# x laid out by features on the host, the first projection fed earlier, later group statistics, and one convolution tap on ACT

## The chip, the core and the metric

The kernel runs on one core of a Trainium2 chip. The core has a matrix engine (TensorE, PE; PEld is its weight load), a vector engine (VectorE, DVE), an activation engine (ScalarE, ACT), a general engine (GpSimd, POOL) and a sync engine (SP), whose queue issues most loads. Each engine runs its instructions in the order in which they were laid down. Engines share an on-chip memory; matmuls write into eight PSUM banks. The metric is the device time of one execution in microseconds (us), here the median of three.

## What is computed

One layer over a sequence of 2048 tokens with 1024 features. The input is normalised and modulated by a conditioning vector, projected once into three groups of heads (a gated LRU, HGRN2 and Mamba-2 SSD), and all results go through one output projection, a gate, the residual and a last normalisation:

```python
mod = cond @ w_ada[l] + b_ada[l]
shift, scale, gate = jnp.split(mod, 3, axis=-1)
h = rmsnorm(x, norm_w[l]) * (1.0 + scale[:, None]) + shift[:, None]
u = h @ w_in[l]
a_x, a_g, hg_q, hg_f, hg_i, hg_g, ssd_z, ssd_xbc, ssd_dt = jnp.split(u, split_points, axis=-1)
xa = causal_conv(a_x, ...)                  # width 4, also over ssd_xbc
ya = rg_lru(xa, ...) * jax.nn.silu(a_g)
yb = rmsnorm(hgrn2_chunked(...), hg_norm_w[l]) * jax.nn.silu(hg_g)
yc = rmsnorm(ssd_chunked(...) * jax.nn.silu(ssd_z), by 2 groups)
y = jnp.concatenate([ya, yb, yc], axis=-1) @ w_out[l]
x = x + gate[:, None] * y
return rmsnorm(x, final_norm_w)
```

## The kernel before

Tokens are taken in four blocks of 512 (`tb` 0 to 3), features in eight tiles of 128 (`KT`). The program has two halves, blocks 0 and 1, then 2 and 3. In each half the stages follow one another: the HGRN heads (projections `ps_f`, `ps_q`, `ps_g`, `ps_v`), the SSD groups (`ps_bc`, `ps_x`, `ps_z`), and four LRU stages `i` = 0 to 3 (`ps_lx`, `ps_lg`, then the gates `ps_r`, `ps_i`). After both halves the output stage runs over 16 token tiles and four families of input features, `po` on PE (line 1095).

Every projection is done in a pair of numbers, a high and a low part, in three passes over eight feature tiles: 24 matmuls of 512 tokens for one 128-column block (`proj_mm`, `PASSES`). A weight tile is loaded as `raw`; `split` (line 139) makes `w` or `wt`, high on ACT and low on POOL.

The h tiles are made by `h_tile` (line 307). A tile of x is loaded with tokens on the partitions (`load_x`, line 274), its squares are summed on ACT (`norm_stats`, line 282), it is scaled by the reciprocal root (`norm_scale`, line 293), transposed by four PE matmuls into `ps_xt` (line 311), modulated on ACT (`hf`), cast on DVE to the high part and subtracted on DVE or POOL to the low part (`ht`).

The modulation has 16 numbers per partition in `gsc`. `mod_dma` (line 412) loads 256-column pieces `wta` of `w_ada`; `mod_acc` (line 421) multiplies and adds them on DVE into `macc`; `mod_col` (line 434) sums over the partitions by a matmul with ones into `psm` and adds the constants.

Order. PE's order is written out by hand. For the startup the string `PROG` (line 40) lists the steps: D, A and C are loads, accumulation and column sums of one modulation tile, X loads a block of x, S and N its statistics and scaling, H builds h tile k of block tb, M runs the three projections on it, w and W load and split the first weights, K loads constants (`consts`, line 452), B starts the other weight loads. Later `weave` (line 366) mixes a list of projection pieces with branches, generators which hand over after each step, by given weights: `pend` holds the branches that run beside the next stage. The other engines' orders come from a scheduler that places each operation when the program is built. ACT operations made by `sact` (line 151) keep their written order. The loads on the sync queue use eight lanes: a load waits for the one eight before it.

`conv` (line 494) copies the last three columns of the block before (`halo`) into `craw` on DVE, the projection into it on ACT, and then runs four taps on DVE (one `tensor_scalar`, line 500, and three multiply-adds, line 72) into `cacc`. `stats` (line 509) sums the squares of a group over partitions by `pq` matmuls (line 513) after POOL has added up `acc`. `lru` (line 810) makes the gate matmuls `ps_r` and `ps_i` for the two blocks, the first pair in the PSUM tag "sc" and the second in "ms"; between them it hands over with weight `L0` = 0.01. In LRU stage 2 of the first half block 2 of x is loaded and scaled (`norm_gen`, line 869), in stage 3 block 3; `h_build` (line 876) makes block 2's h tiles beside stage 3 and block 3's beside the first `ps_v` of the second half. `finish` (line 1116) multiplies a token tile by the gate on POOL, adds the residual and squares.

PSUM tags: "mm" has three banks, "sc" two, "oy" one, "ms" two. Slots of the on-chip memory: 32 temporary tiles, 8 weight slots (`wp`), 16 h slots (`hp`).

## Time and profile before

| | |
|---|---|
| time, median of 3 | 1758.56 us (1758.46 to 1760.5) |
| the profiled execution | 1758.94 us |
| its span | 1757.2 us |
| mean granted PE clock | 0.983 |
| PE busy | 1675.2 us (95%) |
| DVE, POOL, ACT busy | 1149.1, 836.8, 622.3 us |

The span runs from the first to the last recorded instruction of the core; the execution's own time is a little longer. Busy time counts instructions that do work, not waits, branches or the issue of loads. "Granted clock" is the share of full speed at which PE was clocked. In a timeline a row gives start, length, engine, line, operation, output and inputs by name, the tile, the number of instructions, and in brackets how long the engine was idle before it and what released it.

### The profile page before, as it was taken

The page shows a single profiled execution, that of the slowest core. Times are in us where ns is not written, and L with a number is a line of the kernel's source. Part 1 is how long each engine was busy: PE and PEld are TensorE (multiplying, and loading weights), DVE is VectorE, ACT ScalarE, POOL GpSimd, SP SyncE. Part 2 cuts the span into 40 slices and gives each one's busy share as a digit, 9 for nine tenths or more (in the row PEclk, how much of TensorE's full clock was granted, in tenths as well). Part 3 has the DMA queues.
Part 4 walks back from the last instruction along what each step waited for, and adds up shares of the span by engine and source line. Part 5 has one row for each costly group of instructions (what it writes and reads, how often), then busy time and mean ns, then how long its engine had stood idle before and what let it go on. Part 6 is the DMA issues. An engine that isn't in the chain of part 4 may idle for free. (4 is left out here: it accounts for less than half of the span.)

```text
span 1757.2 us, 29508 instructions
## 1 busy us (share of the span) xinstructions
PE 1675.2 (95%) x11448; PEld 1371.7 (78%) x11448; DVE 1149.1 (65%) x2260; ACT 622.3 (35%) x1164; POOL 836.8 (48%) x681
## 2 busy tenths in 40 slices
PE   3899999999999999899999999999999799999998
PEld 2688877788788877788988788788877577888886
DVE  6955756788878947726755778878869636333333
ACT  5322322233333367622322333333446533222221
POOL 3433344265636665424334346634757546333333
PEclk9899999999999999999999999999999899999999
DMA  8612011111202232311120111201224444333332
GB/s 242 166 52 61 26 37 32 34 45 49 73 19 61 66 109 85 89 40 41 29 59 26 37 37 49 84 13 53 69 80 142 135 129 141 94 96 96 92 91 70
DMA packets 178988, 129.52 MB, mean 74 GB/s; under 512 B 13856, under 2 KB 153632, under 8 KB 178848
## 3 DMA queue, kind: packets, MB, share of 16 engines
q1 hardware_dynamic: 142512, 102.72, 20.8%
q10 hardware_dynamic: 33936, 17.04, 3.2%
q0 software_dynamic: 2400, 7.87, 1.1%
q8 instruction: 90, 1.47, 0.4%
q14 instruction: 50, 0.41, 0.1%
...
## 5 line engine op out<-in xcount | busy, mean ns | idle before, releaser
L1095 PE MATMUL po<-wo,yy 128*128 128x512 f32 x1512 | 356.1, 397 | 4.0 <-POOL yy L69 3.4
L69 POOL TENSOR_TENSOR w<-raw,w 128x512 fp32r<-128x512 f32 x158 | 227.2, 1456 | 247.6 <-ACT w L66 232.4
L1095 PEld LDWEIGHTS po<-wo,yy 128*128 128x128 f32 x1512 | 285.5, 189 | 74.5 <-POOL yy L69 4.7
L72 DVE SCALAR_TENSOR_TENSOR cacc<-craw,col,cacc 128x512 f32<-128x512 f32 x192 | 201.9, 1051 | 2.1
L323 PE MATMUL ps_x<-ht,w 128*128 128x512 f32 x768 | 191.2, 397 | 0.0
L323 PE MATMUL ps_z<-ht,w 128*128 128x512 f32 x768 | 189.6, 399 | 0.0
L323 PEld LDWEIGHTS ps_z<-ht,w 128*128 128x128 f32 x768 | 141.9, 188 | 33.6 <-issue 2.1
L323 PEld LDWEIGHTS ps_x<-ht,w 128*128 128x128 f32 x768 | 143.1, 189 | 30.1
L72 DVE SCALAR_TENSOR_TENSOR o<-po,rstd,o 128x512 f32<-128x512 f32 x64 | 47.5, 751 | 116.8 <-PE po L1095 108.0
L69 POOL TENSOR_TENSOR hg_k<-hg_k,hg_t 128x256 f32<-128x256 f32 x80 | 59.5, 759 | 127.1 <-PE ps_sA L551 63.5
L329 PE MATMUL ps_v<-vw,ht 128*128 128x264 f32 x768 | 105.3, 295 | 4.6 <-DVE ht L69 3.6
L66 ACT ACTIVATE w<-raw 128x512 fp32r<-128x512 f32 x158 | 91.4, 625 | 46.0 <-issue 22.3
L323 PE MATMUL ps_f<-ht,w 128*128 128x512 f32 x384 | 101.0, 410 | 6.4 <-DVE ht L315 5.9
L69 POOL TENSOR_TENSOR yy<-yr,yy 128x512 fp32r<-128x512 f32 x61 | 78.5, 1306 | 59.7 <-ACT yy L66 44.2
L323 PE MATMUL ps_bc<-ht,w 128*128 128x512 f32 x384 | 106.0, 417 | 0.0
L329 PEld LDWEIGHTS ps_v<-vw,ht 128*128 128x128 f32 x768 | 99.0, 195 | 7.6 <-DVE ht L69 4.6
L323 PE MATMUL ps_lx<-ht,w 128*128 128x512 f32 x384 | 99.8, 411 | 0.0
L323 PE MATMUL ps_q<-ht,w 128*128 128x512 f32 x384 | 99.7, 407 | 0.0
L69 POOL TENSOR_TENSOR s_ce<-s_ce,cacc 128x512 f32<-128x512 f32 x64 | 96.9, 1532 | 0.8 <-ACT s_ce L66 0.8
L323 PE MATMUL ps_lg<-ht,w 128*128 128x512 f32 x384 | 93.7, 398 | 0.0
L323 PE MATMUL ps_g<-ht,w 128*128 128x512 f32 x336 | 91.9, 408 | 0.0
L323 PEld LDWEIGHTS ps_lx<-ht,w 128*128 128x128 f32 x384 | 72.8, 191 | 20.7 <-issue 5.5
...
## 6 DMA issues: line engine op xcount, KB each, us to landing
...
```

The lines of the kernel that those rows point to most:

```text
L66: S.activation(o, i, f, **kw)
L69: e.tensor_tensor(o, a, b, op=op)
L72: V.scalar_tensor_tensor(o, a, s, b, op0=op0, op1=op1)
L323: d_ = PE.matmul(ps, b.hl[wl][:, k, :], ht[:, hl, :], start=(k == 0 and n == 0), stop=(k == KT - 1 and n == 2))
L329: d_ = PE.matmul(ps[:, 0:264], ht[:, hl, c * P:(c + 1) * P], b.vw[k // 4][wl][:, k % 4, :], start=(k == 0 and n == 0), stop=(k == KT - 1 a ...
L1095: PE.matmul(pss[t, n], yys[u, t][yl][:, k4, :], wts[4 * fam + k4][wl][n], start=(k4 == 0 and i == 0), stop=(k4 == 3 and i == 2))
```

## The change

The diff has ten parts.

1. The host hands over x also transposed (`x_t`), the modulation weights in 2-KB rows (`w_mod`) and the gate's columns apart (`w_gate`). `load_x` reads `x_t` with features on the partitions, so PE transposes nothing. `h_tile` becomes: `h_pre` on DVE (x times the modulation scale times a row `rb` of reciprocal roots), ACT adds the shift and writes the high part, DVE makes the low part. `rb` is made by four 128x128 matmuls against the identity (`norm_rows`, `ps_rb`) and a copy on ACT.
2. Statistics of blocks 0 and 1: ACT squares the eight tiles, DVE adds them up (`xsq`), four matmuls with ones give the sums (`ps_ss`). For blocks 2 and 3 `norm_stats` reads x a second time (16 loads `xr`) and squares it on ACT in LRU stages 0 and 1 of the first half.
3. `mod_acc` on DVE is replaced by `mod_mm`: eight matmuls per modulation tile with `condz` (32 columns, one of them not zero) in four column groups, and a copy on ACT.
4. `PROG` is new. Block 0's x lies in weight slots that are not in use yet, the squares in h slots; U steps are matmuls of ones by ones (`warm`); the first half of the first weights is split on DVE.
5. `conv`: the copies of the halo and the fourth tap move to ACT, which reads PSUM twice; DVE keeps three multiply-adds.
6. `late`: the statistics of an SSD group run one stage later.
7. The first run of the second half holds `ps_v`, `ps_f` and `ps_q` of block 2, then those of block 3; the branches beside it are in parts (`some`), and `norm_gen` hands over three times.
8. The last LRU hands over with weight 5, so that 45 instead of 3 `po` matmuls stand between its two pairs; both pairs use "sc".
9. `finish` multiplies by the gate on DVE.
10. `split` can run on DVE and be told what to follow.

At the start PE's order was this (`psm` are the column sums of the modulation, `ps_xt` transposed x, `ps_f`, `ps_q` and `ps_g` projections of one h tile):

```order
L438 MATMUL psm<-ones,macc 128x1 x2
L311 MATMUL ps_xt<-ident,xt 128x128 x4
L323 MATMUL ps_f<-ht,w 128x512 x3
L323 MATMUL ps_q<-ht,w 128x512 x3
L323 MATMUL ps_g<-ht,wt 128x512 x3
L438 MATMUL psm<-ones,macc 128x1 x2
L311 MATMUL ps_xt<-ident,xt 128x128 x12
L323 MATMUL ps_f<-ht,w 128x512 x3
L323 MATMUL ps_q<-ht,w 128x512 x3
L323 MATMUL ps_g<-ht,wt 128x512 x3
```

and is now this (`warm` are matmuls of ones, `ps_ss` and `ps_rb` the sums and the row of roots):

```order
L997 MATMUL warm<-ones 128x512 x8
L440 MATMUL psm<-wta,condz 32x256 x8
L997 MATMUL warm<-ones 128x512
L449 MATMUL psm<-ones,macc 128x1 x2
L997 MATMUL warm<-ones 128x512 x2
L311 MATMUL ps_ss<-ones,xsq 128x1 x4
L320 MATMUL ps_rb<-ident,xsc 128x128 x4
L440 MATMUL psm<-wta,condz 32x256 x8
L997 MATMUL warm<-ones 128x512
L449 MATMUL psm<-ones,macc 128x1 x2
L440 MATMUL psm<-wta,condz 32x256 x8
L338 MATMUL ps_f<-ht,w 128x512 x3
```

Eight matmuls against `wta` now stand on PE for each modulation tile, four matmuls per h tile are gone, and the first projection stands behind three modulation tiles.

On DVE, in the startup, a stretch before reads like this (`macc` is the accumulation of a modulation tile, `gsc` its two columns, `ht<-hf` the cast to the high part):

```order
L72 SCALAR_TENSOR_TENSOR macc<-wta,cond,macc 128x256
L315 CAST ht<-hf 128x512
L72 SCALAR_TENSOR_TENSOR macc<-wta,cond,macc 128x256
L69 TENSOR_TENSOR gsc<-psm,col 128x1
L72 SCALAR_TENSOR_TENSOR gsc<-psm,col 128x1
L72 SCALAR_TENSOR_TENSOR macc<-wta,cond,macc 128x256
L69 TENSOR_TENSOR gsc<-gsc,col 128x1
```

No `macc` is left there now. At the passage from block 0 to block 1 the order is now this (`xsq` are the sums of squares of block 1, `aneg` is made of the constants `rowp`, the last load of `consts`; `xt<-xt,gsc,rb` is `h_pre`, `ht<-xt,gsc,ht` the low part, `hg_q` and `hg_f` gate operations of block 0):

```order
L480 COPY cs_576<-p_575 128x4
L483 TENSOR_SCALAR e_574<-col 128x4
L488 TENSOR_SCALAR aneg<-aneg 128x16
L305 TENSOR_TENSOR xsq<-xsq 128x512
L72 SCALAR_TENSOR_TENSOR xt<-xt,gsc,rb 128x512
```

and, some 15 operations on a few columns later, this:

```order
L72 SCALAR_TENSOR_TENSOR xt<-xt,gsc,rb 128x512
L69 TENSOR_TENSOR sp_p<-sp_p,sp_w 128x4
L72 SCALAR_TENSOR_TENSOR xt<-xt,gsc,rb 128x512 x7
L136 TENSOR_SCALAR sp_p<-sp_p 128x4
L72 SCALAR_TENSOR_TENSOR hg_q<-hg_q,omlb,ps_q 128x512
L533 TENSOR_SCALAR hg_f<-hg_f,omlb 128x512
L72 SCALAR_TENSOR_TENSOR ht<-xt,gsc,ht 128x512
```

All eight `h_pre` of block 1 stand ahead of its first low part, with two operations of block 0 between.

At the end of the first half PE's order was this (stage 3 of the LRU, then `ps_v` of block 2):

```order
L311 MATMUL ps_xt<-ident,xt 128x128 x4
L323 MATMUL ps_lg<-ht,w 128x512 x6
L815 MATMUL ps_r<-cacc,wab 128x512
L816 MATMUL ps_i<-cacc,wab 128x512
L329 MATMUL ps_v<-vw,ht 128x264 x6
L815 MATMUL ps_r<-cacc,wab 128x512
L816 MATMUL ps_i<-cacc,wab 128x512
L329 MATMUL ps_v<-vw,ht 128x264 x24
L311 MATMUL ps_xt<-ident,xt 128x128 x4
L329 MATMUL ps_v<-vw,ht 128x264 x6
L311 MATMUL ps_xt<-ident,xt 128x128 x4
L329 MATMUL ps_v<-vw,ht 128x264 x12
```

and is now this:

```order
L338 MATMUL ps_lg<-ht,w 128x512 x24
L826 MATMUL ps_r<-cacc,wab 128x512
L827 MATMUL ps_i<-cacc,wab 128x512
L344 MATMUL ps_v<-vw,ht 128x264 x6
L320 MATMUL ps_rb<-ident,xst 128x128 x4
L344 MATMUL ps_v<-vw,ht 128x264 x90
L338 MATMUL ps_f<-ht,w 128x512 x24
L338 MATMUL ps_q<-ht,w 128x512 x6
L826 MATMUL ps_r<-cacc,wab 128x512
L827 MATMUL ps_i<-cacc,wab 128x512
L338 MATMUL ps_q<-ht,w 128x512 x18
L344 MATMUL ps_v<-vw,ht 128x264 x96
```

The transposes are gone; a `ps_rb` stands between the `ps_v`, and the `ps_f` and `ps_q` of block 2 stand ahead of the `ps_v` of block 3 (x96).

The diff, cut to its core:

```diff
-PROG = ("D0 A00 X0 D1 A10 w0 A01 S0 X1 N0013 A11 C0 H00v W0 M00 D2 S1 C1 H01v N10 H10 A20 D3 w1 "
-        "A30 A21 A31 H11v M01 C2 D4 N111g H02 M10 H12 M11 W1 C3 N01 A40 H03 A41 D5 M02 H13 M12 C4 "
-        "A50 H04 D6 A51 M03 A60 H14 D7 M13 C5 H05 H15 A61 M14 M04 C6 K A70 H06 M05 A71 H16v M15 "
-        "C7 B H07v H17 M06 M07 M16 M17")
+PROG = ("X0 D0 w0 D1 w1 D2 S0 U8 A0 U1 C0 U2 R0 W0 D3 A1 U1 C1 H00 D4 W1 A2 M00 C2 H01 D5 A3 M01 C3 H02 D6 A4 M02 C4 "
+        "H03 D7 A5 M03 C5 H04 X1 A6 M04 C6 H05 S1 A7 M05 C7 H06 K M06 H07 R1 B M07 H10 H11 M10 H12 M11 H13 M12 H14 M13 "
+        "H15 M14 H16 M15 H17 M16 M17")
...
-    def load_x(tb):
-        r = [[tmp("xt") for _ in range(2)] for _ in range(4)]
+    def load_x(tb, ts=None):
+        r = []
+        for k in range(KT):
+            t_ = ts[k // 2][:, k % 2] if ts else tmp("xt")
+            nc.sync.dma_start(t_, x_t[k * P:(k + 1) * P, tb * TB:(tb + 1) * TB])
+            r.append(t_)
...
+    def norm_stats(tb):
+        st = tmp("xst", (P, 2, 4), bufs=2)
         for n in range(2):
             for i in range(4):
                 r0 = tb * TB + i * P
-                nc.sync.dma_start(r[i][n], x[r0:r0 + P, n * TB:(n + 1) * TB])
-        return r
-
-    def norm_stats(xs):
-        st = tmp("xst", (P, 2, 4), bufs=2)
-        for n in range(2):
-            for i in range(4):
-                sq = tmp("xsq", (P, TB), BF16, bufs=1)
-                act(sq, xs[i][n], AF.Square, accum_out=st[:, n, i:i + 1])
+                xr = tmp("xr")
+                nc.sync.dma_start(xr, x[r0:r0 + P, n * TB:(n + 1) * TB])
+                act(xr, xr, AF.Square, accum_out=st[:, n, i:i + 1])
...
+    def norm_sum(xs, sqs):
+        a = sqs[0][:, 0]
+        for k in range(KT):
+            sq = sqs[k // 2][:, k % 2]
+            act(sq, xs[k], AF.Square)
+            if k > 0:
+                d_ = V.tensor_tensor(a, a, sq, op=ADD)
+        return a, d_.ins.name
+
+    def norm_cols(a):
+        ps = bank(ps_ms, "ms", "ps_ss")
+        for i in range(4):
+            PE.matmul(ps[:, i:i + 1], a[:, i * P:(i + 1) * P], ones[:, 0:1], start=True, stop=True)
+        st = tmp("xsc", (P, 4), bufs=2)
+        sact(st, ps[:, 0:4], AF.Sqrt, scale=1.0 / D, bias=epsc[:, 0:1])
+        V.reciprocal(st, st)
         return st
 
-    def norm_scale(xs, st, n, on_act=()):
+    def norm_rows(st):
+        ps = bank(ps_ms, "ms", "ps_rb")
         for i in range(4):
-            if on_act is G:
-                tt(G, xs[i][n], xs[i][n], st[:, 0, i:i + 1].to_broadcast([P, TB]), MUL)
-            elif i in on_act:
-                act(xs[i][n], xs[i][n], AF.Copy, scale=st[:, 0, i:i + 1])
-            else:
-                V.tensor_scalar(xs[i][n], xs[i][n], st[:, 0, i:i + 1], None, op0=MUL)
-
-    def norm_x(xs, on_act=()):
-        st = norm_stats(xs)
-        for n in range(2):
-            norm_scale(xs, st, n, on_act)
-
-    def h_tile(xs, k, dep=None, lo=G):
+            PE.matmul(ps[:, i * P:(i + 1) * P], st[:, i:i + 1].to_broadcast([P, P]), ident, start=True, stop=True)
+        rb = tmp("rb")
+        d_ = S.activation(rb, ps, AF.Copy)
+        return rb, d_.ins.name
+
+    def h_pre(xs, rb, k):
+        stt(xs[k], xs[k], gsc[:, 1, k:k + 1], rb, MUL, MUL)
+
+    def h_tile(xs, k, dep=None):
         ht = hp.tile([P, 2, TB], F32R, tag="h", name="ht")
-        ps = bank(ps_ms, "ms", "ps_xt")
-        for i in range(4):
-            d_ = PE.transpose(ps[:, i * P:(i + 1) * P], xs[i][k // 4][:, (k % 4) * P:(k % 4 + 1) * P], ident)
-            after(d_, dep)
-        hf = tmp("hf")
-        act(hf, ps, AF.Identity, scale=gsc[:, 1, k:k + 1], bias=gsc[:, 0, k:k + 1])
-        V.tensor_copy(ht[:, 0], hf)
-        tt(lo, ht[:, 1], hf, ht[:, 0], SUB)
+        after(S.activation(ht[:, 0], xs[k], AF.Identity, bias=gsc[:, 0, k:k + 1]), dep)
+        stt(ht[:, 1], xs[k], gsc[:, 0, k:k + 1], ht[:, 0], ADD, SUB)
         return ht
...
+            wt = tmp("wta", (P, 2, 2 * P))
+            nc.sync.dma_start(wt, w_mod[j, :, q * TB:(q + 1) * TB].rearrange("p (k c) -> p k c", k=2))
...
+    def mod_mm(j):
+        psm = bank(ps_ms, "ms", "psm")
+        for k in range(KT):
+            r = k % 4
+            PE.matmul(psm[32 * r:32 * r + 32, 0:2 * P], condz[:, k, :], mws[j][k // 2][:, k % 2],
+                      start=k < 4, stop=k >= 4)
+        mas[j] = tmp("macc")
+        act(mas[j][:, 0:2 * P], psm[:, 0:2 * P], AF.Copy)
...
     def conv(ps, wi, wname, bname, i):
         raw = tmp("craw", (P, TB + 3))
-        V.tensor_copy(raw[:, 0:3], halo[:, wi, :])
+        act(raw[:, 0:3], halo[:, wi, :], AF.Copy)
         act(raw[:, 3:], ps, AF.Copy)
-        V.tensor_copy(halo[:, wi, :], raw[:, TB:TB + 3])
         a = tmp("cacc")
-        V.tensor_scalar(a, raw[:, 0:TB], cc(wname, 4 * i), cc(bname, i), op0=MUL, op1=ADD)
-        for k in (1, 2, 3):
+        act(a, ps, AF.Identity, scale=cc(wname, 4 * i + 3), bias=cc(bname, i))
+        act(halo[:, wi, :], ps[:, TB - 3:TB], AF.Copy)
+        for k in range(3):
             stt(a, raw[:, k:k + TB], cc(wname, 4 * i + k), a, MUL, ADD)
...
-    def lru(i, tbs, xa, gs):
+    def lru(i, tbs, xa, gs, l0=L0):
         r, ig = {}, {}
         for n, tb in enumerate(tbs):
-            pool, tag = ((ps_sc, "sc"), (ps_ms, "ms"))[n]
+            pool, tag = ((ps_sc, "sc"), (ps_ms, "ms"))[n if l0 < 1 else 0]
...
-                yield L0
+                yield l0
...
+    def norm_gen(xs, st):
+        rb, _ = norm_rows(st)
         yield
+        for k in range(KT):
+            h_pre(xs, rb, k)
+            if k % 4 == 3:
+                yield
+
+    def some(g, n):
+        for w_ in itertools.islice(g, n):
+            yield w_
...
-                ps_ = pv(tbs[0])
                 if p == 0:
-                    brs = pend + [(h_build(tbs[1], xs_next, HTS[tbs[1]], hdep[tbs[1]]), 8)]
-                    run(ps_, brs)
-                    pend = []
-                    ps_ = pv(tbs[1])
+                    g_ = pend[0][0]
+                    run(pv(tbs[0]) + pf(wf, h, tbs[0]) + pq_(wq, h, tbs[0]),
+                        [(some(g_, 1), L0), (norm_gen(xs_next, xst[1]), 3),
+                         (h_build(tbs[1], xs_next, HTS[tbs[1]], hdep[tbs[1]]), 8), (some(g_, 9), 3)] + pend[1:])
+                    run(pv(tbs[1]) + pf(wf, h, tbs[1]) + pq_(wq, h, tbs[1]) + pg(wg, h, tbs[0]) + pg(wg, h, tbs[1]))
...
+            pend = [(ssd_bc(g, tb, bc[0, tb], bc[1, tb], dts[tb][1], bcg), 3) for tb in tbs] + late
+            late = []
...
-            pend += [(stats(acc[tb], 1 + g, tb), 2) for tb in tbs]
-        hdep = {}
+            late = [(stats(acc[tb], 1 + g, tb), 2) for tb in tbs]
+        hdep, xst = {}, {}
...
+            if i < 2 and half == 0:
+                xst[i] = norm_stats(2 + i)
             if i == 2 and half == 0:
                 xs_ = load_x(2)
-                pend += [(norm_gen(xs_), 1)]
+                pend += [(norm_gen(xs_, xst[0]), 3)]
...
-                    norm_x(xs_next)
...
+            l0 = 5 if i == 3 and half == 1 else L0
+            pend = [(lru(i, tbs, xa, gs, l0), 3 + l0)] + late
+            late = []
...
-            tt(G, o, o, gate[n], MUL)
+            tt(V, o, o, gate[n], MUL)
```

More of the change, by code (lines that the diff above doesn't have):

```diff
@@ L1 @@
+import itertools
 from contextlib import ExitStack
@@ L95, in trunk @@
     cond = cpool.tile([P, 8], F32, name="cond")
+    condz = cpool.tile([P, 8, 32], F32, name="condz")
     dhalf = cpool.tile([P, 8], F32, name="dhalf")
@@ L437, in mod_col @@
         for i in range(2):
-            PE.matmul(psm[:, i:i + 1], ma[:, i], ones[:, 0:1], start=True, stop=True)
-        tt(V, gsc[:, 0, j:j + 1], psm[:, 0:1], cc("b_shift", j), ADD)
+            PE.matmul(psm[:, i:i + 1], ma[:, i * P:(i + 1) * P], ones[:, 0:1], start=True, stop=True)
         stt(gsc[:, 1, j:j + 1], psm[:, 1:2], 1.0, cc("b_scale", j), ADD, ADD)
         tt(V, gsc[:, 1, j:j + 1], gsc[:, 1, j:j + 1], cc("norm_w", j), MUL)
+        tt(V, gsc[:, 0, j:j + 1], psm[:, 0:1], cc("b_shift", j), ADD)
     G.memset(wab, 0.0)
@@ L945, in trunk @@
                         for tb in tbs}
-                xsb, sts, u_ = {}, {}, None
+                xsb, sts, u_, dn, rn = {}, {}, None, None, None
+                sqs = [[hp.tile([P, 2, TB], F32, tag="h", name="xsq") for _ in range(4)] for _ in tbs]
+                x0s = [wp.tile([P, 2, TB], F32, tag="w", name="xt") for _ in range(4)]
                 for op_ in PROG.split():
                     o_, ar = op_[0], [int(c) for c in op_[1:] if c.isdigit()]
-                    e_ = V if op_[-1] == "v" else G
                     if o_ == "D":
@@ L970, in trunk @@
                         for b_ in WBL[0:3]:
-                            b_.parts(ar[0])
+                            b_.parts(ar[0], *((dn, V) if ar[0] == 0 else (rn, G)))
+                    elif o_ == "U":
+                        pu = bank(ps_ms, "ms", "warm", (P, 4, P))
+                        for _ in range(ar[0]):
+                            PE.matmul(pu, ones, ones.unsqueeze(1).to_broadcast([P, 4, P]), start=True, stop=True)
                     elif o_ == "K":
@@ L1195, in trunk @@
     tc_pe.__exit__(None, None, None)
-_INS = ["x", "w_ada", "w_in", "w_out", "wa", "wx", "cols", "rows", "ident", "tri", "masks", "onehot"]
+_INS = ["x", "x_t", "w_mod", "w_gate", "w_in", "w_out", "wa", "wx", "cols", "rows", "ident", "tri", "masks", "onehot"]
 def _arrays(inp):
```

85 lines of the change are left out of this document (38 added, 47 removed).

## The prediction

> **What bounds the kernel now.** I read the page first (busy shares), then the waits of the matrix engine PE, then busy time by windows, then PE's timeline at the places that these point to.
>
> ```profile
> PE 1675.2 (95%) x11448; PEld 1371.7 (78%) x11448; DVE 1149.1 (65%) x2260; ACT 622.3 (35%) x1164; POOL 836.8 (48%) x681
> ```
>
> PE is busy 1675.2 of the 1757.2 us of the span, so it is idle for 82.0 us. No other engine is near its limit over the whole span. Removing DVE or POOL work is therefore worth only the PE idle time that it ends. The view of PE's waits says who ends that idle time (total us, times, longest):
>
> ```profile
> PE psm L438 <- DVE macc L72: 14.6, 4, 10.6
> PE ps_xt L311 <- DVE xt L300: 10.8, 5, 7.4
> PE ps_r L815 <- DVE cacc L72: 8.3, 1, 8.3
> PE pq L513 <- POOL acc L69: 5.6, 4, 2.0
> PE po L1095 <- POOL yy L69: 3.4, 3, 2.5
> ```
>
> Almost all of it is in few places. Busy time of PE in windows (start:end, length, PE busy, weight loads, DVE, ACT, POOL, granted PE clock, DMA share, GB/s) shows where:
>
> ```profile
> 0.00:50.00 50.00, 19.98 (x66) 14.85 (x67) 32.23 (x68) 23.43 (x52) 16.07 (x19) 0.90 0.79 229
> ...
> 100.00:150.00 50.00, 50.00 (x593) 44.82 (x592) 24.41 (x53) 12.10 (x34) 18.60 (x20) 1.00 0.10 27
> ...
> 700.00:750.00 50.00, 43.38 (x270) 37.67 (x269) 37.92 (x60) 29.77 (x57) 23.24 (x17) 0.92 0.41 107
> 1350.00:1400.00 50.00, 41.06 (x158) 30.56 (x157) 40.01 (x46) 31.16 (x45) 32.02 (x24) 0.90 0.33 107
> ```
>
> A steady window is full at clock 1.00. Three stages are not: the startup (first 95 us), the passage from the first half to the second (690 to 752), and the last LRU before the output stage (1350 to 1400). There the clock falls as well. The sum goes stage by stage.
>
> **Startup, term 1: 14 us less.** The timeline of PE (start, length, line, operation; in brackets the idle time before):
>
> ```profile
> 10.56 1.01 PE L438 MATMUL psm<-ones,macc 128*128 128x1 f32 x4 [10.56 <-DVE macc L72]
> ...
> 25.98 0.80 PE L323 MATMUL ps_f<-ht,w 128*128 128x512 f32 x1 [5.94 <-DVE ht L315]
> ...
> 82.28 1.12 PE L311 MATMUL ps_xt<-ident,xt 128*128 128x128 f32 x4 [4.18 <-DVE gsc L72]
> ...
> 90.98 0.86 PE L323 MATMUL ps_f<-ht,w 128*128 128x512 f32 x3
> ...
> 92.36 0.85 PE L323 MATMUL ps_g<-ht,wt 128*128 128x512 f32 x3
> ```
>
> The first projection runs from 25.98 to about 93.1. Its 16 steps of three groups need 2.08 us each (from 90.98 to 92.36 are two groups, 0.69 each), 33 us in all; half the stretch is waiting on DVE, which computes the modulation (64 `macc` operations). The change gives that to PE and removes the transposes. What is late next is the data, then a row of DVE work. In the changed order on the sync queue the second block of x is the 54th large load; with 32 modulation tiles, 16 of x and 6 of weights, 256 KB each, 14.2 MB have to land. Rates, from the same view of windows:
>
> ```profile
> 10.00:20.00 10.00, 2.09 (x8) 1.54 (x8) 3.84 (x14) 7.46 (x20) 0.00 (x0) 1.00 1.02 314
> ...
> 24.00:26.00 2.00, 0.02 (x1) 0.02 (x1) 1.97 (x4) 1.94 (x5) 0.79 (x1) 1.00 1.04 392
> 30.00:36.00 6.00, 3.30 (x13) 2.22 (x12) 4.56 (x8) 0.78 (x1) 4.17 (x4) 0.94 1.01 267
> ```
>
> The 30:36 window carries modulation weights in 512-byte runs at 267 GB/s; 24:26 carries x in 2-KB runs at 392. The change makes the modulation runs 2 KB too, so I take 370 from between 314 and 392: 38.3 us, and with some 4 us before the stream starts it ends at 42.5 (41 to 49). The Trainium skill's page "DMA: Bandwidth & Descriptors" (Bandwidth) gives about 358 GB/s as the limit of one core from HBM; by it the stream would take 39.6 us and this term would be 1.3 us smaller. The 392 GB/s of the second row exceeds that figure, and the measurement decides.
>
> Behind that stream stand small loads: 8 loads are in flight, so `rowp` is issued only when x has landed. DVE's order has `aneg`, which needs `rowp`, ahead of the last square-sum of the second block. `rowp` takes 3.5 us to land (first row below), so the chain stands at 46.
>
> ```profile
> DMA to landing us min/median/max: 3.5/3.5/3.5
> ...
> L72 DVE SCALAR_TENSOR_TENSOR cacc<-cacc,dhalf,ps_y 128x512 f32<-128x512 f32 x32 | 23.5, 744 | 11.9 <-PE ps_y L783 11.9
> ...
> L151 ACT ACT_TABLE_LOAD x29 | 37.2, 1283 | 8.7 <-POOL l_gs L69 8.3
> ```
>
> From there: one addition, one h operation, a root with its table load (1.283), the row broadcast on PE and its copy on ACT, about 6 us to 52; then eight `h_pre` in a row by 0.72 to 0.744, 5.8 us, to 57.6; two gate operations ahead of the first `lo`, and that `lo`, 2 us, to 59.6. Eight steps of 2.08 plus some 2 us at half clock end at 78 to 79, against 93.1. Bounds: 72 if DVE's small operations slip by, 88 if the stream runs at 314 and the row of DVE work meets POOL; gain 5 to 21, taken 14.
>
> The new modulation matmuls (eight per step, 32 columns each, in four column groups) have no row of their own. Nearest: a 128x512 f32 matmul is two records, 0.43 apart (the last two rows).
>
> ```profile
> 104.01 0.76 PE L551 MATMUL ps_sA<-hg_q,hg_k 128*32 128x32 f32 x64
> ...
> 406.05 0.39 PE L783 MATMUL ps_y<-s_ce,s_st 128*64 128x128 f32 x4
> 406.27 0.39 PE L778 MATMUL ps_y<-s_m,s_xdt 128*64 128x128 f32 x4
> ...
> 421.36 1.05 PE L754 MATMUL ps_bx<-s_xw,s_btok 128*128 128x128 f32 x8
> ...
> 710.25 1.02 PE L815 MATMUL ps_r<-cacc,wab 128*128 128x512 f32 x2
> 711.11 1.02 PE L816 MATMUL ps_i<-cacc,wab 128*128 128x512 f32 x2
> ```
>
> 710.25 to 711.11 is 0.86 for 512 columns, so 0.43 for 256. One after another, eight cost 3.4 us; four at a time, 0.86. Halves do overlap: four records of 64 columns start 0.22 apart (0.055 each), where eight of 128 columns take 0.81 (0.10 each). So I take 0.86, which the loads of each step (4 of 256 KB, 2.8 us at 370) cover beside 2.08 of projection. The page "TensorEngine Tiling (Array Packing)" of the Trainium skill (Key Properties) says that a switch of tiling mode drains TensorE, which speaks against these 8 detours. The 100:150 window holds five groups of 32-column matmuls (the first is the 104.01 row) between projections, with PE busy 50.00 of 50: here the trace does not agree, a switch shows no idle time. By the trace a step costs 0.86; by the page each detour would add two drains of unknown length.
>
> **Passage to the second half, term 2: 13 us less.** PE's timeline:
>
> ```profile
> 697.82 1.11 PE L311 MATMUL ps_xt<-ident,xt 128*128 128x128 f32 x4 [3.90 <-ACT hf L66]
> 698.58 2.71 PE L323 MATMUL ps_lx<-ht,w 128*128 128x512 f32 x6
> ...
> 718.28 1.49 PE L329 MATMUL ps_v<-vw,ht 128*128 128x264 f32 x10 [1.72 <-DVE ht L69]
> 719.61 0.60 PE L311 MATMUL ps_xt<-ident,xt 128*128 128x128 f32 x4
> 719.97 0.98 PE L329 MATMUL ps_v<-vw,ht 128*128 128x264 f32 x6
> ...
> 738.06 0.39 PE L329 MATMUL ps_v<-vw,ht 128*128 128x264 f32 x1 [1.15 <-DVE ht L69]
> 739.47 0.81 PE L329 MATMUL ps_v<-vw,ht 128*128 128x264 f32 x2 [1.02 <-DVE ht L315]
> ```
>
> From the first of these gaps (3.90) there are nine, the last of 0.19 at 740.47, 10.5 us in all. Half clock after the 3.90 costs some 1.5 more: those transposes take 1.11 against 0.60 at 719.61, and the six `ps_lx` (2.71) about 1.0 over six at full clock (6 x 0.23 and the end of the last). A group of four transposes occupies PE for 0.36 (719.61 to 719.97); 16 groups are 5.8. The change takes all three away: the statistics come from a second reading of x two LRU stages earlier, and h no longer passes through PE. It adds two broadcasts of four 128x128 matmuls, 0.81 each by the `ps_bx` row (eight records), 1.6. The new h tile is DVE 0.744, ACT 0.6, DVE 0.744 (the `cacc<-cacc,dhalf,ps_y` row and the ACT row below), where DVE had a scaling, a cast and a subtraction: about as much DVE time. Its cover is longer for the last block: 48 more matmuls (11 us) stand behind its first values. I leave 3 us of waits: 10.5 + 1.5 + 5.8 - 1.6 - 3 = 13.2. Ends: 17 with none, 4 if the DVE chain still sets the pace and only the transposes are saved.
>
> **Last LRU, term 3: 10 us less.**
>
> ```profile
> 1381.36 2.07 PE L815 MATMUL ps_r<-cacc,wab 128*128 128x512 f32 x2 [8.29 <-DVE cacc L72]
> ...
> 1388.10 4.21 PE L1095 MATMUL po<-wo,yy 128*128 128x512 f32 x17 [0.66 <-ACT l_r L151]
> ```
>
> PE has three output matmuls to run and then waits 8.29 for the second convolution; 0.66 follows, and half clock costs 2.9 (`ps_r` 2.07 against 1.02 at 710.25, and likewise `ps_i` and the six `po` up to the second wait). With 45 matmuls ahead (45 x 0.23 = 10.4 us) the convolution is covered. The second group's output tiles must then be there earlier; I charge 2 us: 8.3 + 0.7 + 2.9 - 2 = 9.9. Ends: 12, or 4 if the output tiles are late.
>
> **Late statistics, term 4: 6 us less.** Four waits for the POOL sum, 5.6 in all, one of which left `pq` at half clock (1.86 against 1.05): 6.4. They move behind another stage's branches, some 20 us later. Ends 3 and 7.
>
> **Gate multiplication from POOL to DVE, term 5: 2.5 us less.** The chain at 1461 has `o` ahead of `yy` on POOL (start, length):
>
> ```profile
> 1461.09 1.72 POOL o L69
> 1462.81 1.75 POOL yy L69
> ```
>
> and PE waits 2.55 of the 3.4 for that `yy`. DVE, 65% busy over the span, has the room. Ends 0 and 3.4.
>
> **Convolution: nothing.** It trades a DVE operation and two copies for one more 512-wide ACT pass and small copies.
>
> ```profile
> L66 ACT ACTIVATE xsq<-xt 128x512 bf16<-128x512 f32 x32 | 20.1, 627 | 6.1 <-DMA xt<-in_x 5.5
> L66 ACT ACTIVATE craw<-ps_x 128x512 f32<-128x512 f32 x32 | 19.1, 597 | 47.4 <-PE ps_x L323 37.4 <-issue 10.0
> ```
>
> By 0.597 (second row) plus two copies of three columns, which I estimate at 0.2 each, each of the 64 costs ACT 1 us; a projection of 24 matmuls lasts 5.5 us on PE and three banks take turns, so this lies beside PE. Without that cover it is rival C.
>
> **A new wait, term 6: 2 us more.** In LRU stages 0 and 1 of the first half ACT squares eight tiles (0.627 each by the `xsq` row, with the read of the sum 0.8, so 6.6 us) after loads that it must wait for, and behind them in its in-order stream stand the copies that free the small PSUM banks. Bounds 0 and 6.
>
> Sum: 14 + 13.2 + 9.9 + 6.4 + 2.5 - 2 = 44.0. The profiled execution took 1758.94 (span 1757.2 and 1.7 around it), 0.4 above the median of 1758.56; 1758.9 - 44 = 1715.
>
> **The rivals.** A: the startup keeps its length. For it: the new chain is long, with loads, two table loads and eight DVE operations in a row, and if column groups run one at a time each step grows by 2.6 us, 8 x 2.6 = 20 against a cover of 8 x 0.7, so the end comes near 91. Against: the pairs at 406.05. Gain 2 instead of 14: 1727.
> B: the passage keeps its stall. The waits named are for DVE and ACT, in order behind LRU work that meets POOL; the h tiles still go through both. Gain 1 instead of 13: 1727. Against: the statistics and a table load leave the path. A and B together: 1739.
> C, the slower side: ACT's longer convolution holds the PSUM banks, and PE waits at each. With 44 us gained elsewhere, it decides from 44/64 = 0.69 us of PE wait per convolution; at the whole 1 us it is 64 - 44 = 20 us slower: 1779. Against: ACT is busy 35%.
> D: no remaining waits at all, startup end at 74, no term 6: 5 + 3 + 2 + 2 = 12 more: 1703.
> E: the moves only shift waits and nothing is gained: 1758.
>
> **Chances.** Forecast 0.42, A 0.20, B 0.15, both 0.07, D 0.09, C 0.05, E 0.02. About 0.2% (3.5 us) is what a measurement of this kernel can tell from no change. All but C and E are faster: 0.93; E the same: 0.02; C slower: 0.05. The range leaves out C, E, half of D and the upper end of both together: 1702 to 1739. The forecast's own range is 1708 to 1723.
>
> **What would show it.** Right: PE ends its first projection near 78; eight `psm` matmuls take about 0.86; no `ps_xt`; idle time between 690 and 745 of the old scale under 4 us; `ps_r` of the last LRU without a wait; `pq` not in the list of waits. Wrong: `psm` at 3.4 us a step (A), PE waiting for `ht` by 1 us at each tile (B), PE waiting for ACT `craw` or `cacc` throughout (C), or waits behind `xr` squares longer than 6 us (term 6).

## The result, and the profile after

The changed kernel takes 1719.17 us (median of 4, 1718.6 to 1721.23) against 1759.53 for the kernel before: ratio 0.9773, 95% interval 0.9756 to 0.979. The forecast was 1715 with a range of 1702 to 1739. The profiled execution after took 1718.6 us, its span is 1716.8, 40.4 less than the 1757.2 of before.

The page after, first lines (busy time, share and number of instructions by engine):

```profile
span 1716.8 us, 29450 instructions
...
PE 1669.7 (97%) x11520; PEld 1362.3 (79%) x11520; DVE 1083.1 (63%) x2042; ACT 669.7 (39%) x1346; POOL 768.3 (45%) x630
```

PE's idle time fell from 82.0 to 47.1 us, and its busy time by 5.5. Idle time that is filled isn't all gained time, though: ahead of the first projection, which starts no earlier than before, PE was busy 2.13 of 25.98 us and is now busy 22.14 of 25.85, most of it with `warm` matmuls. No kernel without these was run. The waits of PE after (total us, times, longest):

```profile
PE ps_r L826 <- DVE cacc L72: 7.7, 1, 7.7
PE ps_f L338 <- DVE ht L72: 4.9, 2, 4.6
PE ps_v L344 <- DVE dtr L379: 4.8, 1, 4.8
PE ps_f L338 <- ACT ht L330: 2.4, 2, 1.5
```

The long waits of before for `macc`, `xt`, `hf`, `gsc` and the POOL sum are gone. The three longest that remain have one thing in common, as DVE's timeline shows further down: DVE has eight `h_pre` ahead of what PE waits for.

The starts of the stages in PE's two timelines give where the time came from. "To" means the first instruction of that name; the LRU of the first half ends at the second `ps_lx` of stage 3 (690.08 before, with its transposes, and 685.18 after).

| stretch | before, us | after, us | less | forecast |
|---|---|---|---|---|
| startup, to `ps_v` | 96.4 | 86.0 | 10.4 | 14 |
| HGRN, first half | 187.5 | 185.8 | 1.7 | 0 |
| SSD, first half | 308.0 | 303.3 | 4.7 | 6.4 with the second |
| LRU, first half | 98.2 | 110.1 | -11.9 | -2 |
| passage, to `ps_g` of the second half | 84.2 | 68.5 | 15.7 | 13.2 |
| HGRN, second half | 176.2 | 176.3 | -0.1 | 0 |
| SSD, second half | 310.7 | 304.9 | 5.8 | (above) |
| LRU, second half, to the 147th recorded `po` | 160.4 | 149.1 | 11.3 | 9.9 |
| rest of the output stage | 335.5 | 332.8 | 2.7 | 2.5 |

Startup and LRU fell short by 14 us, and stretches that were costed at less or nothing made up for 10 of them. The 1.7 of the HGRN stretch is no gain to build on: a second profile of the changed kernel (the control below) has 187.4 there, as before. Rows of PE's timeline after, the startup first:

```profile
28.47 1.07 PE L440 MATMUL psm<-wta,condz 128*32 128x256 f32 x16
29.47 0.96 PE L338 MATMUL ps_f<-ht,w 128*128 128x512 f32 x3
...
59.47 0.50 PE L338 MATMUL ps_f<-ht,w 128*128 128x512 f32 x1 [0.85 <-ACT ht L330]
64.61 1.22 PE L338 MATMUL ps_f<-ht,w 128*128 128x512 f32 x2 [4.64 <-DVE ht L72]
...
82.16 0.85 PE L338 MATMUL ps_g<-ht,wt 128*128 128x512 f32 x3
```

The first projection starts at 25.85 as before (25.98) but then has only five waits, 9.2 us in all, of which 4.64 is the longest; block 1's first low part is 5 us later than the 59.6 of the forecast. What DVE does ahead of that low part (`ht<-xt,gsc,ht`):

```profile
55.79 0.75 DVE L72 SCALAR_TENSOR_TENSOR xt<-xt,gsc,rb 128x512 f32<-128x512 f32 x1 [0.57 <-ACT rb L322]
...
56.53 4.72 DVE L72 SCALAR_TENSOR_TENSOR xt<-xt,gsc,rb 128x512 f32<-128x512 f32 x7
61.17 1.24 DVE L136 TENSOR_SCALAR sp_p<-sp_p 128x4 f32<-128x4 f32 x1
62.33 0.73 DVE L72 SCALAR_TENSOR_TENSOR hg_q<-hg_q,omlb,ps_q 128x512 f32<-128x512 f32 x1
62.98 0.92 DVE L533 TENSOR_SCALAR hg_f<-hg_f,omlb 128x512 f32<-128x512 f32 x1
63.82 0.74 DVE L72 SCALAR_TENSOR_TENSOR ht<-xt,gsc,ht 128x512 fp32r<-128x512 f32 x1
```

Then PE in the LRU, the passage and the last LRU:

```profile
670.06 2.07 PE L826 MATMUL ps_r<-cacc,wab 128*128 128x512 f32 x2 [7.74 <-DVE cacc L72]
...
712.65 5.07 PE L344 MATMUL ps_v<-vw,ht 128*128 128x264 f32 x24 [4.78 <-DVE dtr L379]
...
1347.06 9.32 PE L1126 MATMUL po<-wo,yy 128*128 128x512 f32 x39 [0.78 <-DVE l_gs L69]
1357.07 1.13 PE L826 MATMUL ps_r<-cacc,wab 128*128 128x512 f32 x2 [0.69 <-ACT l_r L152]
```

The 8.29 before the last `ps_r` has become 0.69. In its place there is a wait in stage 2 of the first half. What DVE does there:

```profile
660.93 7.41 DVE L72 SCALAR_TENSOR_TENSOR xt<-xt,gsc,rb 128x512 f32<-128x512 f32 x8
...
668.33 1.68 DVE L72 SCALAR_TENSOR_TENSOR cacc<-craw,col,cacc 128x512 f32<-128x512 f32 x1
```

Eight `h_pre` of block 2 stand ahead of the last tap of the convolution that PE waits for. At the passage it is the same with the eight of block 3, ahead of the copy `dtr`:

```profile
702.33 9.53 DVE L72 SCALAR_TENSOR_TENSOR xt<-xt,gsc,rb 128x512 f32<-128x512 f32 x8
...
712.44 0.15 DVE L379 COPY dtr<-ps_v 128x8 f32<-128x8 f32 x1
```

### The profile page after: what moved, and what is told of

It reads as the page before. It is cut to its first block, busy times and chain, and to the rows that moved or that the text cites. A ratio compares the mean times of both kernels' runs of the same rounds, so it can differ in the third digit from the quotient of the medians.

```text
span 1716.8 us, 29450 instructions
## 1 busy us (share of the span) xinstructions
PE 1669.7 (97%) x11520; PEld 1362.3 (79%) x11520; DVE 1083.1 (63%) x2042; ACT 669.7 (39%) x1346; POOL 768.3 (45%) x630
## 4 chain that ended last, share of the span: by engine, by line
PE 84%; ACT 4%; DVE 4%; DMA 3%; issue 3%; POOL 2%; SPq 0%; ACTq 0%; POOLq 0%; DVEq 0%
PE po L1126 19%; PE ps_z L338 10%; PE ps_x L338 10%; PE ps_v L344 5%; PE ps_f L338 5%; PE ps_g L338 5%; PE ps_bc L338 5%; PE ps_q L338 4%; PE ps_lx L338 3%; PE ps_lg L338 2%; PE ps_y L789 2%; PE ps_bx L765 2%; PE ps_y L794 1%; PE ps_sA L562 1%; DVE xt L72 1%
## 5 line engine op out<-in xcount | busy, mean ns | idle before, releaser
L69 POOL TENSOR_TENSOR w<-raw,w 128x512 fp32r<-128x512 f32 x156 | 223.5, 1451 | 209.3 <-ACT w L141 191.0
L72 DVE SCALAR_TENSOR_TENSOR cacc<-craw,col,cacc 128x512 f32<-128x512 f32 x192 | 205.9, 1079 | 47.7 <-ACT cacc L66 38.3
L344 PE MATMUL ps_v<-vw,ht 128*128 128x264 f32 x768 | 99.6, 290 | 4.8 <-DVE dtr L379 4.8
L338 PE MATMUL ps_bc<-ht,w 128*128 128x512 f32 x384 | 101.2, 405 | 0.0
L338 PEld LDWEIGHTS ps_f<-ht,w 128*128 128x128 f32 x384 | 70.9, 191 | 26.3 <-DVE ht L72 5.6
```

The lines of the kernel that those rows point to most:

```text
L69: e.tensor_tensor(o, a, b, op=op)
L72: V.scalar_tensor_tensor(o, a, s, b, op0=op0, op1=op1)
L338: d_ = PE.matmul(ps, b.hl[wl][:, k, :], ht[:, hl, :], start=(k == 0 and n == 0), stop=(k == KT - 1 and n == 2))
L344: d_ = PE.matmul(ps[:, 0:264], ht[:, hl, c * P:(c + 1) * P], b.vw[k // 4][wl][:, k % 4, :], start=(k == 0 and n == 0), stop=(k == KT - 1 a ...
```

## Experiments

Each kernel is the changed kernel with one edit, timed beside runs of the kernel before (medians 1756.06, 1756.7 and 1755.81 in the three groups). Differences are those of the ratios to the kernel before, times 1756. Only `consts_late`, `gate_pool` and `conv_dve` share the control's group. The changed kernel itself had 0.9773 in its first measurement and 0.9796 as the control, which is 4 us, so a difference of that size between groups needs a stage that shows it.

| kernel | median, us | ratio (95%) | against control, us |
|---|---|---|---|
| control | 1721.08 | 0.9796 (0.9783 to 0.981) | 0 |
| lru_order | 1714.99 | 0.976 (0.9744 to 0.9776) | -6.3 |
| pass_order | 1715.3 | 0.9758 (0.9741 to 0.9776) | -6.7 |
| start_order | 1717.71 | 0.9775 (0.9759 to 0.9792) | -3.7 |
| all_order | 1709.94 | 0.9731 (0.9713 to 0.9748) | -11.4 |
| consts_late | 1715.11 | 0.9762 (0.9749 to 0.9775) | -6.0 |
| all_and_consts | 1705.76 | 0.9707 (0.9688 to 0.9727) | -15.6 |
| gate_pool | 1722.98 | 0.9808 (0.9795 to 0.9822) | +2.1 |
| stats_now | 1722.27 | 0.9802 (0.9775 to 0.9829) | +1.1 |
| l0_small | 1729.1 | 0.984 (0.982 to 0.986) | +7.7 |
| conv_dve | 1729.31 | 0.9847 (0.9834 to 0.9861) | +9.0 |
| mod_one_group | 1734.76 | 0.987 (0.985 to 0.9889) | +13.0 |

**control.**

> The changed kernel itself, unaltered, run beside the next three so that they can be compared with it in one place. Expected: the ratio to the kernel before again 0.977 (0.975 to 0.979).

The ratio is 0.9796, just above the range that was expected. Nearly all of the difference in span to the first profile lies in the startup, 90.1 us to `ps_v` instead of 86.0. Windows from 30 to 40 us, of the changed kernel and of the control:

```profile
30.00:40.00 10.00, 10.00 (x82) 7.42 (x84) 5.16 (x16) 2.73 (x6) 0.00 (x0) 1.00 1.04 388
```

```profile
30.00:40.00 10.00, 10.00 (x86) 7.41 (x84) 5.13 (x16) 2.71 (x5) 0.00 (x0) 1.00 0.95 314
```

The loads ran at 388 GB/s in the one and 314 in the other (last column), and `rowp`, behind them, was issued at 44.35 and at 47.19. Of the eight profiles with this startup unaltered, two had 314 in this window and reach `ps_v` at 89.5 and 90.1; six had 366 to 391 and reach it at 85.7 to 88.2. The HGRN stretch behind it varies too, from 185.8 to 187.4. From there on a stretch that an edit doesn't touch agrees to about 1 us (SSD 303.3 in six of them). So single stages are compared below, besides the medians.

**The three orders on DVE.** `lru_order` puts the last tap ahead of block 2's `h_pre`; the others make `h_pre` two tiles ahead of the low part:

```diff
 # lru_order: the last convolution's name is kept in cl[0]
-            h_pre(xs, rb, k)
+            h_pre(xs, rb, k, cl[0])
 # pass_order, in h_build (the h_pre of block 3 leave norm_gen)
+            if tb == 3:
+                h_pre(xs, rbs[id(xs)], k, los.get((id(xs), k - 2)))
 # start_order
-                        h_pre(xsb[ar[0]], sts[ar[0]], ar[1])
+                        h_pre(xsb[ar[0]], sts[ar[0]], ar[1], los.get((id(xsb[ar[0]]), ar[1] - 2)))
```

> One row of the changed kernel is moved: the last multiply-add of the second convolution of LRU stage 2 (first half) is put ahead of the eight h_pre of block 2 on DVE. The computation is complete. Theory (order): the 7.74 us for which PE waits there for cacc, and the 2.5 us of half clock behind it, come from the eight h_pre that stand ahead of that row; PE's wait falls under 1 us and the time from 1719 to about 1709. Rival (DVE is short of time there): the h tiles of block 2 come later by the same amount, PE waits for ht in stage 3 instead, and the time stays within 3 us of 1719.

PE's timeline of this kernel:

```profile
665.83 1.13 PE L829 MATMUL ps_r<-cacc,wab 128*128 128x512 f32 x2
...
710.11 5.65 PE L346 MATMUL ps_v<-vw,ht 128*128 128x264 f32 x24 [7.15 <-DVE dtr L381]
```

The wait of 7.74 is gone, and the LRU stretch is 101.0 instead of 110.1: the order of one row was its cause. But 2.4 of it come back at the passage, where the wait for `dtr` is 7.15 instead of 4.78. Some 6 us by the medians, 4 to 5 over both stretches: the theory holds for the wait, the rival for a part of the time.

> In the changed kernel the eight h_pre of block 3 are made two tiles ahead of their low parts, instead of all eight in a row, so that the dtr copies of ps_v come between them on DVE. The computation is complete. Theory (order): the 4.78 us wait of PE for dtr goes, the time falls by 3 to 5 us to about 1715. Rival (DVE is short of time): the low parts of the last tiles come later, PE waits for ht or dtr in smaller pieces, and the time stays within 2 us of 1719.

```profile
711.00 3.20 PE L347 MATMUL ps_v<-vw,ht 128*128 128x264 f32 x24 [1.46 <-DVE dtr L382]
```

The wait falls from 4.78 to 1.46, the passage from 68.5 to 63.4. The theory holds, and this 5.1 of the stage is a safer figure than the 6.7 of the medians.

> In the changed kernel the h_pre of block 1 in the startup are made two tiles ahead of their low parts, instead of seven in a row. The computation is complete. Theory (order): the first low part of block 1 comes 4 to 6 us earlier, PE's wait of 4.64 us falls under 1, the first projection ends near 77 instead of 82.9 and the time is about 1714. Rival (the row is only in front): one tile then costs DVE 1.5 us plus small operations against 2.08 on PE, with POOL in the way; PE waits at several tiles and the end stays at 81 to 83.

By the medians 3.7 us with overlapping intervals. The projection ends at 82.2 instead of 83.0: the rival. DVE and POOL in that kernel's timeline:

```profile
59.16 0.75 DVE L331 SCALAR_TENSOR_TENSOR ht<-xt,gsc,ht 128x512 fp32r<-128x512 f32 x1
59.82 1.78 DVE L326 SCALAR_TENSOR_TENSOR xt<-xt,gsc,rb 128x512 f32<-128x512 f32 x1
61.52 1.50 DVE L69 TENSOR_TENSOR hg_t<-hg_f 128x256 f32<-128x256 f32 x1
```

```profile
59.25 1.80 POOL L69 TENSOR_TENSOR hg_q<-hg_q,hg_f 128x512 f32<-128x512 f32 x1 [9.35 <-DVE sp_p L136]
61.01 6.05 POOL L69 TENSOR_TENSOR vw<-raw,vw 128x512 fp32r<-128x512 f32 x4
```

The first tile came early, but then POOL began its work on `hg_q` and the v weights, and the next `h_pre` took 1.78 instead of 0.75. PE's wait moved to the second tile, where it is 3.67.

> All three orders at once (last convolution ahead of the h_pre of block 2; h_pre of blocks 1 and 3 two tiles ahead of their low parts). The computation is complete. Theory (order): the three gains add up, 10 + 4 + 5 = 19 us, to about 1700. Rival (DVE is short of time): less than 8 us, 1711 or more.

11.4 us by the medians: between the two. The LRU and passage stretches together are 170.0 instead of 178.6 (177.6 in the control), 8 to 9 less; a wait for `dtr` of 3.9 stays. `ps_v` starts at 87.1, within the spread of the unaltered startup, so the stages show no gain there.

**Constants later in the startup.**

```diff
-... H06 K M06 H07 R1 B M07 H10 H11 M10 H12 ...
+... H06 M06 H07 R1 M07 H10 H11 M10 K B H12 ...
```

> In the changed kernel's startup the step that loads and prepares the constants stands after the first projection step of block 1 (M10) instead of before M06, so that aneg, the table loads for the exponentials and the small operations on four columns leave the chain that ends in the row rb of block 1. The computation is complete. Theory (chain): of the 3.5 us by which this chain was later than forecast most comes back, the first low part of block 1 comes 3 to 6 us earlier than 64.6, the first projection ends at 77 to 79 and the time is 4 to 5 us under the control. Rival (POOL): the length of the DVE operations behind rb, doubled while POOL works on the v weights, sets the time; the projection ends at 82 to 83 and the time is within 2 us of the control.

6.0 us less. DVE's timeline of this kernel, then PE's:

```profile
52.89 5.39 DVE L72 SCALAR_TENSOR_TENSOR xt<-xt,gsc,rb 128x512 f32<-128x512 f32 x8 [1.88 <-ACT rb L322]
```

```profile
59.00 0.78 PE L338 MATMUL ps_f<-ht,w 128*128 128x512 f32 x2 [3.07 <-DVE ht L72]
...
81.89 1.08 PE L562 MATMUL ps_sA<-hg_q,hg_k 128*32 128x64 f32 x32 [4.03 <-POOL hg_q L69]
```

The row of `h_pre` starts 2.9 us earlier (52.89 against 55.79), the first low part 5.6 (59.00 against 64.61), and the projection ends at 77.3, where the theory put it. The other 2.7 are the three operations that no longer stand between: `sp_p`, `hg_q` and `hg_f`, 61.17 to 63.82 in the rows above. The edit also moves step B, the loads of the other weights, and POOL gets its first full v weights later, at 69.47 instead of 60.50. So this kernel doesn't separate the constants from POOL: `sp_p` took 1.24 beside POOL's work, where others of its row took 0.17. A part of the gain goes into the next wait: `hg_q` now stands behind the small operations, 4.03 instead of 1.83.

**Both together**, with the softplus for the LRU taken out of that step:

```diff
 # in consts, with the three lines around it
-        softplus(cpos[:, 1], e4, 4)
...
 # called after the first heads
+    def consts_lru():
+        e5 = tmp("e5", (P, 4), bufs=1)
...
+        softplus(cpos[:, 1], e5, 4)
```

> The three DVE orders of all_order, the constants after the first step of block 1, and the softplus on four columns (cpos) taken out of that step, so that it runs in DVE's idle time at the start. The computation is complete. Theory (the remaining waits are DVE's and ACT's order): the gains add up, 11 us of all_order and 6 or more of consts_late, so 17 to 20 us under the control's 0.9796 of the kernel before: ratio 0.969 to 0.970. Rival (they share the same time): ratio 0.973 as with all_order alone.

1705.76 us, faster than both kernels, 15.6 less than the control; the theory's sum was 17 to 20. LRU and passage take 168.0, the startup 80.3, with the 4.05 wait for `hg_q` left.

**The gate on POOL again.**

```diff
-            tt(V, o, o, gate[n], MUL)
+            tt(G, o, o, gate[n], MUL)
```

> The multiplication by the gate in the output stage goes back from DVE to POOL; all else is the changed kernel. The computation is complete. Theory (term 5 of the prediction): PE's waits for yy behind o on POOL come back, 2.5 us (0 to 3.4) over the control. Rival: the 5 us by which the output stage got shorter come from this part alone through the half clock behind those waits, and the time is 5 us over the control.

2.1 us, with overlapping intervals. The rest of the output stage is 334.6, against 331.5 to 333.6 in the others, and PE's waits for `yy` are 3.2 instead of the control's 1.6. That agrees with term 5, whose 2.5 is hardly more than the spread.

**Statistics not late.**

```diff
-            late = [(stats(acc[tb], 1 + g, tb), 2) for tb in tbs]
+            pend += [(stats(acc[tb], 1 + g, tb), 2) for tb in tbs]
```

> The statistics of an SSD group run beside the next stage again, as before the change, instead of one stage later; all else is the changed kernel. The computation is complete. Theory (late statistics): the waits for the POOL sum (5.6 us before) come back together with half clock behind the two that are 2 us long (2 us each), 8 to 10 us over the control. As forecast (term 4, with 0.8 us of half clock): 6.4 us over it. Rival (another part, as the tap on ACT, took these waits away): under 2 us.

The waits of PE for the POOL sum in this kernel:

```profile
PE pq L524 <- POOL acc L69: 1.9, 4, 0.9
```

1.9 us instead of 5.6, and no half clock behind them. 1.1 us in all by the medians, 1.8 and 1.4 in the two SSD stretches, with the LRU stretch 1.2 shorter: the rival. With the rest of the change, the sums come early enough without being put later. Windows of the kernel before, behind its two waits of 2.03 and 2.02 us for that sum (470.69 and 1137.84), show a lower granted clock, 0.83 and 0.66:

```profile
470.00:480.00 10.00, 9.31 (x44) 7.85 (x45) 7.48 (x11) 3.62 (x8) 3.81 (x4) 0.83 0.14 43
1136.00:1146.00 10.00, 8.16 (x30) 7.02 (x31) 6.22 (x7) 2.54 (x6) 3.96 (x3) 0.66 0.18 53
```

That is 1.7 and 3.4 us of clock. In `stats_now` the longest such wait is 0.9, and the windows around its waits (460 to 470 and 1118 to 1128) have 1.00.

**The last LRU with weight 0.01.**

```diff
-            l0 = 5 if i == 3 and half == 1 else L0
+            l0 = L0
```

> The last LRU hands over with weight 0.01 again, so that 3 instead of 45 output matmuls stand between its two pairs and the second pair uses the banks ms; all else is the changed kernel. The computation is complete. Theory (term 3): PE waits some 8 us for cacc at the second pair and loses 2 to 3 us at half clock, 8 to 11 us over the control, ratio 0.984 to 0.986. Rival (the output matmuls then run without the waits that they have now, or the convolution with a tap on ACT is early enough): under 3 us over the control.

```profile
1349.07 1.88 PE L826 MATMUL ps_r<-cacc,wab 128*128 128x512 f32 x2 [2.54 <-DVE cacc L72]
...
1358.68 16.83 PE L1126 MATMUL po<-wo,yy 128*128 128x512 f32 x63 [4.54 <-ACT l_r L152]
```

7.7 us; this stretch is 158.3 instead of 149.6, 8.8. The convolution is now 6 us earlier than before the change (2.54 instead of 8.29), and what is missed lies in the second wait and the half clock. Term 3 holds in size; the theory's wait of 8 us for `cacc` isn't there, most of it is now the 4.54 for `l_r`.

**The convolution on DVE again.**

```diff
-        act(raw[:, 0:3], halo[:, wi, :], AF.Copy)
+        V.tensor_copy(raw[:, 0:3], halo[:, wi, :])
...
-        act(a, ps, AF.Identity, scale=cc(wname, 4 * i + 3), bias=cc(bname, i))
-        act(halo[:, wi, :], ps[:, TB - 3:TB], AF.Copy)
+        V.tensor_copy(halo[:, wi, :], raw[:, TB:TB + 3])
+        V.tensor_scalar(a, raw[:, 0:TB], cc(wname, 4 * i), cc(bname, i), op0=MUL, op1=ADD)
...
-        for k in range(3):
+        for k in (1, 2, 3):
```

> The convolution goes back to four taps and the two copies on DVE with one ACT pass; all else is the changed kernel. The computation is complete. Theory (prediction, convolution at nothing): within 2 us of the control. Rival 1 (ACT's longer convolution holds PE up in places): up to 5 us faster than the control. Rival 2 (DVE needs the room): DVE has 64 operations of 0.75 us and 128 copies more; where DVE already lags, in the first half's LRU stages and at the passage, PE waits longer for cacc and dtr, and the time is 5 to 15 us over the control.

The wait of PE for the last tap of the first half's LRU in the control (total us, times, longest):

```profile
PE ps_r L826 <- DVE cacc L72: 7.5, 1, 7.5
```

The waits of PE in this kernel:

```profile
PE ps_r L826 <- DVE cacc L72: 9.1, 1, 9.1
PE ps_v L344 <- DVE dtr L379: 5.2, 1, 5.2
...
PE po L1126 <- DVE l_gs L69: 4.5, 1, 4.5
```

9.0 us slower: rival 2. The passage with the LRU before it takes 181.2 instead of 177.6, the last LRU 153.5 instead of 149.6, the second SSD stretch 1.2 more. There PE waits for DVE, and what a convolution adds on DVE does not lie beside other work: 0.72 us for a tap (`tensor_scalar`) and 0.49 and 0.45 for its two copies, as means of 64.

**One column group.**

```diff
-            r = k % 4
-            PE.matmul(psm[32 * r:32 * r + 32, 0:2 * P], ..., start=k < 4, stop=k >= 4)
+            PE.matmul(psm[0:32, 0:2 * P], ..., start=k == 0, stop=k == 7)
```

> The eight modulation matmuls of a step all go to the first group of 32 columns, one after another, instead of to four groups; the copy and the column sum take 32 partitions. All else is the changed kernel, and the computation is complete. Theory (column groups run beside one another): a step that takes 1.0 us now takes 3.4, the first projection ends 8 to 15 us later than the control's 87, the time is 8 to 15 us over the control. Rival (matmuls of 32 columns are short anyway, or the loads cover them): within 2 us of the control.

```profile
33.35 3.64 PE L439 MATMUL psm<-wta,condz 128*32 128x256 f32 x16
36.92 0.96 PE L338 MATMUL ps_f<-ht,w 128*128 128x512 f32 x3
```

A step takes 3.57 (33.35 to 36.92) instead of 1.00 (28.47 to 29.47), and the kernel 13 us more. The two prices that the prediction worked out, 3.4 and 0.86, were both close, each some 0.15 too low. The page "TensorE: Matmul & The Clock Gate" of the Trainium skill (Part 3, measured speedup) gives 2.38 for three column groups; four groups give 3.6 here.

## Why the prediction was right, point by point

No kernel undoes parts 1, 2, 4 and 7 one at a time, so what is said of them below is read from the traces of before and after.

**What bounds the kernel**: right as to the places. PE's idle time in them could be gained, and removed DVE work counted only there. But idle time was not all of it: in the startup "half the stretch is waiting on DVE" misreads the trace. The first projection's window, of the kernel before and of the changed one (busy time of PE, PEld, DVE, ACT and POOL with counts, granted clock, DMA share, GB/s):

```profile
25.98:93.10 67.12, 54.43 (x232) 42.20 (x232) 60.40 (x147) 24.16 (x45) 31.49 (x25) 0.87 0.66 178
```

```profile
25.85:83.02 57.17, 47.93 (x270) 36.56 (x272) 40.61 (x109) 26.90 (x50) 9.88 (x8) 0.91 0.63 197
```

PE was idle for 12.7 of the 67.1 us. What PE was busy with beyond the 33 us of projection was mostly transposes, column sums and the clock of 0.87. Of the 10 us gained there, 3.4 are idle time and 3.6 the clock (8.7 us lost to it before, 5.1 after); the other 3 are not split further. The forecast's gain was safe from the misreading, because it was worked out from the end of the new course.

**Term 1, startup**: 10.4 instead of 14 (6.3 in the control, with slower loads). The course was as forecast: modulation steps at 1.00, stream, `rowp`, the last sum, eight `h_pre`, the first low part. Mis-sized was "about 6 us to 52": `rowp` was issued at 44.35, `rb` stood at 55.8. In `consts_late`, with the constants out of that chain, the row starts 2.9 earlier, most of these 3.8. Behind it, `sp_p` and `hg_f` were slow beside POOL, which the bounds had named.

**Term 2, passage**: 15.7 instead of 13.2. Idle time and transposes went as counted; 5.0 of waits stayed where 3 were left for them, and only one of the two broadcasts lies in this stretch (0.8 instead of 1.6). Mis-sized was the half clock behind the old gaps: the 1.5 in the forecast is behind the first of them alone. Windows over a run of `ps_v` in the passage (length, busy time of PE, PEld, DVE, ACT, POOL with counts, granted clock, DMA share, GB/s), of the kernel before:

```profile
740.47:751.97 11.50, 11.50 (x76) 11.50 (x77) 1.12 (x5) 1.97 (x7) 0.68 (x1) 0.79 0.71 178
```

and of the changed kernel:

```profile
730.42:742.43 12.01, 11.81 (x97) 11.60 (x95) 8.30 (x11) 5.92 (x11) 7.28 (x6) 1.00 0.03 7
```

At a granted clock of 0.79, 76 matmuls took 11.50 us (0.151 each); at 1.00, 97 took 12.01 (0.124 each). That is 2.1 us over these 76 alone (76 x 0.027), beside the 1.5 counted. Against it stand 2.1 behind the new wait for `dtr`, where 24 `ps_v` take 5.07 (24 x 0.21 against 24 x 0.124). From start to start of PE's matmuls the stretch adds up so: waits 5.5 less (7.5 forecast), transposes 6.1 less (5.8), broadcast 0.8 more, and all other matmuls 4.7 less (1.5), of which `ps_v` are 3.4 and `ps_lx` 1.6. Of these 4.7 the clock explains 1.5 to 2; some 3 us are not assigned to a cause.

**Term 3, last LRU**: 9.9 forecast, 7.7 to 8.8 by undoing it alone. **Term 5, gate**: 2.5 forecast, 2.1 measured, with a spread of that size.

**Term 4, late statistics**: the step failed. The waits did go (SSD stretches 10.5 less together), but undoing the step costs 1 to 3 us, not 6.4: in the new kernel POOL's sum comes almost in time also without it. What the 10.5 consist of is clear: the two waits of 2.0 and 5.1 of half clock behind them make 9.1, where the forecast had taken 0.8 for the half clock. Which part made the sum early is open. Undoing the tap alone costs the SSD 1.2; a kernel with both undone was not run.

**Convolution at nothing**: the step failed, in the kernel's favour. The sentence weighed only ACT's extra 1 us against the cover that PE gives; what DVE gives up was not costed, though in the three places of terms 1 to 3 DVE is what PE waits for. Measured: 9.0 us gained.

**Term 6, a new wait of 2 us**: right in kind and nearly in size. Behind the squares on ACT PE waits 1.1 us (0.76 and 0.34 for `s_ce`, at 580.19 and 582.42), and with the tap moved ahead (`lru_order`) the stretch is 2.8 longer than before, of which the late statistics are some 1.2. Missed was the costly new wait of that stretch, 7.74 and half clock behind it: it came from block 2's `h_pre` ahead of a convolution tap on DVE. The prediction saw such a row in the startup and did not look for it at the other two places.

Of the signs named, `ps_xt` and `pq` are gone from the waits. Three came near and were missed: the first projection ends at 83 instead of near 78, the passage idles 5.0 instead of under 4, and `ps_r` of the last LRU still waits 0.69.

So 44 forecast and 40 measured agree partly by luck: in the first half's LRU 9 us were lost to the order on DVE (110.1 against 101.0 in `lru_order`), the convolution gained 9, and both were left out. Rival A is refuted by the startup, 6 to 10 us shorter; `mod_one_group` shows what its one group at a time would have cost. Rival C (ACT on the path) is refuted by `conv_dve`; of rival B a wait of 4.78 was there.
